# The chunks of an SSD scan in three stages instead of two, with the sample state loaded in mid-group

## The chip, the cores and the metric

The kernel runs on one core of a Trainium2 chip. The metric is the device time of one execution in microseconds (us). The core's engines run side by side and each works through its own instructions in order: PE (TensorE) multiplies matrices and writes to PSUM, DVE (VectorE) and POOL (GpSimd) work elementwise, ACT (ScalarE) computes activations, and SP (SyncE) issues the transfers (DMAs). An instruction that needs what another engine makes waits for a semaphore, and what is queued behind it on its engine waits with it.

## What is computed

One step of a small hybrid encoder: a state-space (SSD) mixer, an MLP, an attention layer and a second MLP, over 1024 prompt tokens and 32 sample tokens of width 1024. The change lies in the SSD mixer, of which the part that matters is the scan over chunks of tokens:

```
def step(h, inp):
    xdt_c, adt_c, b_c, c_c = inp
    a_cs = jnp.cumsum(adt_c, axis=1)
    seg = a_cs[:, :, None] - a_cs[:, None, :]
    decay = jnp.exp(jnp.where(causal[None, :, :, None, None], seg, -jnp.inf))
    cb = jnp.einsum('btgn,bsgn->btsg', c_c, b_c)
    y_diag = jnp.einsum('btsg,btsgr,bsgrp->btgrp', cb, decay, xdt_c)
    y_off = jnp.einsum('btgn,bgrpn,btgr->btgrp', c_c, h, jnp.exp(a_cs))
    decay_end = jnp.exp(a_cs[:, -1:] - a_cs)
    h_new = h * jnp.exp(a_cs[:, -1])[..., None, None] + jnp.einsum(
        'bsgn,bsgr,bsgrp->bgrpn', b_c, decay_end, xdt_c)
    return h_new, y_diag + y_off
```

The state h runs from chunk to chunk of the prompt. The sample tokens start from a state that is an input (h0). There are 8 groups of 4 heads of 64 channels each; a group has its own B and C (128 wide), and its x is two blocks of 128 channels, x0 and x1. B, C, x0 and x1 each come from a projection, a causal convolution of four taps and SiLU. The output y gets D·x added, is multiplied by SiLU(z) (the gate), normalized per group, and projected.

## The kernel before, in words

The scan stage runs from about 83 to 806 us, group by group (g = 0 to 7). A group has nine chunks: eight of 128 prompt tokens, and chunk 8 with the 32 sample tokens. The loop at L601 to L615 makes two lists of small pieces for each g and weaves them (L64 to L76). The main list holds the projections: the two z tiles of group g−1 (`z_tile`), and the four convolution tiles B, C, x0 and x1 of group g+1 (`conv_tile`), with the three pieces of the gate of group g−1 among them. That is 39 pieces in a middle group, and a piece of a projection is 12 matmuls of 128x352. The side list holds the scan of group g (`scan_thunks`), 18 pieces, which are spread evenly, three main pieces behind. Group 0 has the convolutions alone in its main list; group 7 has the z tiles of groups 6 and 7, the gate and the first output projection.

A convolution tile takes three PSUM tiles of 352 columns, which DVE moves out (L400; the last in two parts, L403 and L404). Then `post` runs: the first tap on ACT (L414), two taps on DVE (L416, twice), the last on DVE (L418 and L419), tanh on ACT (L420), and the last product on DVE (L421), whose result, s_4x for block x of group 4, is the operand of group 4's scan. The weights of a projection are split into a high part on ACT (L141) and a low part on POOL (L142). In the gate, PE adds up squares (`ss_g`, L227), DVE takes the inverse root, and L555 scales.

A chunk c of the scan has two stages before. `stage_a(c)` (L453 to L481) loads the cumulated decays (ab), has PE make C·B and three transposes into one PSUM tile (pa, L460 to L463), adds the mask on POOL (L465), takes exp on ACT (L468, four heads), multiplies on DVE (L469, giving L), scales x twice on DVE (L473, giving xd), copies the transposed B on ACT (L476, giving bt), and makes exp(ab)·C on ACT (L478) and POOL (L479). `stage_b(c)` (L483 to L520) makes on PE the state product (L495) into one half of a PSUM bank (tile pb, two buffers), then eight matmuls of outputs into the other half: four with L (L500) and four with the state h of the chunk before (L503). POOL scales the old state (ht, L509), DVE adds the state product (h, L511), and DVE adds D·x to the outputs in place (L514, twice). For chunk 8, the load of h0 is issued in its `stage_b` (L489). The side list runs a(0), a(1), b(0), a(2), b(1) and so on to b(8).

The order in the code is not the order on each engine: a list scheduler of the framework places the instructions of all engines by its own estimate of when they are ready, so a piece that is written at another place can change places with others on its engine. In names, s_3x0 is block x0 of group 3, pb_3_6 is chunk 6 of group 3, and ps_i27 is the projection of column tile 27, which is x1 of group 4 (26 is its x0).

Of the kernel before, what the change touches and what calls it, by code (L numbers as in the profile page):

```python
# [7 lines left out]
F32 = mybir.dt.float32  # L8
# [4 lines left out]
ALU = mybir.AluOpType  # L13
# [28 lines left out]
C_DS = C_AL + 1  # L42
# [50 lines left out]
def hybrid_step(ctx: ExitStack, tc: tile.TileContext, xt, cst, cbf, w_in, w_dt, w_out, w_up0, w_dn0, w_qkv, w_o,  # L93
                w_up1, w_dn1, ssm0, ck, cv, y_o, pssm_o, sssm_o, conv_o, pk_o, v_o):
    nc = tc.nc
    ve, sc, gp, te = nc.vector, nc.scalar, nc.gpsimd, nc.tensor
    dma = nc.sync.dma_start
# [15 lines left out]
    def col(c, n=1):  # L113
        return cs[:, c:c + n]
# [174 lines left out]
    def ssd_layer():  # L289
# [4 lines left out]
        with st:  # L294
            sp = st.enter_context(tc.tile_pool(name="sp", bufs=1))
            qp = st.enter_context(tc.tile_pool(name="qp", bufs=2))
# [89 lines left out]
            slots = {}  # L386
# [60 lines left out]

            def scan_thunks(g):

                out = []  # L450
                box = {}

                def stage_a(c):  # L453
                    w = 128 if c < 8 else 32
                    tk = slice(128 * c, 128 * c + w)
                    B, C, x0, x1 = (slots[g, k] for k in ("B", "C", "x0", "x1"))
                    ab = qp.tile([128, 4, 128], F32, name=f"ab_{g}_{c}", tag="ab", bufs=3)
                    dma(ab[:, :, :w], acs_d[4 * g:4 * g + 4, tk].partition_broadcast(128))
# [3 lines left out]
                    te.transpose(A[0:w, 256:384], x1[:, tk], ident)
                    te.transpose(A[0:w, 384:512], B[:, tk], ident)  # L463
                    L = qp.tile([128, 4, 128], F32, name=f"L_{g}_{c}", tag="L")
                    gp.tensor_tensor(L[0:w, :, :w], ab[0:w, :, :w],  # L465
                                     cs[0:w, None, C_MASK:C_MASK + w].to_broadcast([w, 4, w]), op=ALU.add)
                    for h in range(4):
                        sc.activation(L[0:w, h, :w], L[0:w, h, :w], AF.Exp, bias=naT[0:w, c, 4 * g + h:4 * g + h + 1])  # L468
                    ve.tensor_tensor(L[0:w, :, :w], L[0:w, :, :w], A[0:w, None, 0:w].to_broadcast([w, 4, w]), op=ALU.mult)  # L469
# [6 lines left out]
                    sc.activation(bt[0:w, :], A[0:w, 384:512], AF.Copy)  # L476
                    if c > 0:
                        sc.activation(ab[:, :, :w], ab[:, :, :w], AF.Exp)  # L478
                        gp.tensor_tensor(ab[:, :, :w], ab[:, :, :w],  # L479
                                         C[:, None, tk].to_broadcast([128, 4, w]), op=ALU.mult)  # L480
                    box[c] = (L, xd, bt, ab)  # L481

                def stage_b(c):  # L483
                    w = 128 if c < 8 else 32
                    tk = slice(128 * c, 128 * c + w)
# [9 lines left out]
                    te.matmul(Bp[:, 256:512], bt[0:w, :], xd[0:w, 1, :], start=True, stop=True)  # L495

                    for j in range(2):
                        heads = [(hd, Bp[64 * (hd % 2):64 * (hd % 2) + 64, 128 * j:128 * j + w]) for hd in (2 * j, 2 * j + 1)]
                        for hd, o in heads:
                            te.matmul(o, xd[0:w, 0, 64 * hd:64 * hd + 64], L[0:w, hd, :w], start=True, stop=(h is None))  # L500
                        for hd, o in heads:
                            if h is not None:
                                te.matmul(o, h[:, 64 * hd:64 * hd + 64], ce[:, hd, :w], start=False, stop=True)  # L503
                    hn = qp.tile([128, 256], F32, name=f"h_{g}_{c}", tag="hst", bufs=3)
                    if h is None:
                        ve.tensor_copy(hn, Bp[:, 256:512])
                    else:
                        ht = qp.tile([128, 256], F32, name=f"ht_{g}_{c}", tag="ht", bufs=1)
                        gp.tensor_tensor(ht.rearrange("p (h d) -> p h d", d=64), h.rearrange("p (h d) -> p h d", d=64),  # L509
                                         een[:, 4 * g:4 * g + 4, c, None].to_broadcast([128, 4, 64]), op=ALU.mult)  # L510
                        ve.tensor_tensor(hn, ht, Bp[:, 256:512], op=ALU.add)  # L511
                    for j in range(2):
                        x = slots[g, f"x{j}"]
                        ve.scalar_tensor_tensor(x[:, tk], x[:, tk], col(C_DS + 2 * g + j), Bp[:, 128 * j:128 * j + w],  # L514
                                                op0=ALU.mult, op1=ALU.add)
                    box["h"] = hn
                    if c == 7:
                        dma(pssm_o[g], hn)
                    if c == 8:
                        dma(sssm_o[g], hn)  # L520
# [41 lines left out]
            for d in range(KD):  # L562
                x = hx.tile([128, T], F32, name=f"x0_{d}", tag=f"h{d}")
# [13 lines left out]
            for i, n in enumerate(("ss", "dt", "tails")):  # L577
                ps = p1.tile([128, 512], F32, name=f"p_rstd{i}", tag=n)
                for c in range(2 * i, min(2 * i + 2, 5)):
                    w = 256 if c < 4 else DEC  # L580
# [3 lines left out]
                w = min(512, T - 512 * i)  # L584
# [16 lines left out]
            for g in range(8):  # L601
                main, side = [], scan_thunks(g)
                gt = gate(g - 1) if g > 0 else []
                if g > 0:
                    main += z_tile(g - 1, 0) + z_tile(g - 1, 1)
                if g < 7:
                    for k in ("B", "C", "x0", "x1"):
                        main += gt[0:1] + conv_tile(g + 1, k)
                        gt = gt[1:]
                else:  # L610
                    main += gt[0:1] + z_tile(7, 0) + gt[1:2] + z_tile(7, 1, False) + gt[2:3]
                    out0 = late(lambda: down_block(w_out[0], load_o(yn_d, 0, None, stage(0), 1), X, pg, "o0",
                                                   gmajor=True), 24)
                    main += [lambda: X.extend(load_x(xt, (2, 3, 4, 5, 0, 1, 6, 7), range(2)))] + out0[:6]
                weave(main, side, 2 if g == 7 else 3)  # L615
# [945 lines left out]
    with ExitStack() as st:  # L1561
# [15 lines left out]
        box = {}  # L1577
# [120 lines left out]
```

## Time and profile before

| what | us |
|---|---|
| median of three runs | 3042.72 |
| lowest and highest of them | 3035.66, 3044.68 |
| the profiled execution's own time | 3043.05 |
| its span in the trace | 3041.2 |
| the scan stage (83 to 806): PE busy | 694.54 of 723.00 |
| the same: DVE, ACT, POOL busy | 555.60, 284.32, 445.88 |

The page shows one execution. Busy is the time in which an engine had an instruction under way; matmuls are pipelined, so the time from one's start to the next one's start is shorter than its duration. In a timeline a row gives the start, the duration, the engine, the line, the operation with out<-in, and the count of instructions that it stands for; in brackets is the idle time before it and what ended that.

### The profile page before, as it was taken

The numbers are of one execution on the slowest core, as the hardware profiler recorded it, in microseconds if no ns is written. First come the engines' busy times: TensorE is split into PE (matmuls) and PEld (weight loads), VectorE is DVE, ScalarE is ACT, GpSimd is POOL, SyncE is SP. The second block draws the span as 40 slices with busy tenths as digits, with TensorE's granted clock in tenths as the row PEclk, the third lists the DMA queues.
The fourth block names the chain that finished last, engine by engine and source line by source line (L and its number), as shares of the span: only waits on it lengthen the run. The fifth ranks groups of instructions, "written<-read, shape, count | busy, mean of one in ns | idle before, by whom it ended". The sixth has DMA issues, their size and how long they took to land.

```text
span 3041.2 us, 54987 instructions
## 1 busy us (share of the span) xinstructions
PE 2951.4 (97%) x22206; PEld 2805.2 (92%) x22206; DVE 2272.5 (75%) x3268; ACT 1288.2 (42%) x2207; POOL 768.8 (25%) x591
## 2 busy tenths in 40 slices
PE   9999999999999999999998999999999999999999
PEld 7899888998899999989998988888889999999999
DVE  7877787777847877688777577677777977688776
ACT  4433334333323433344333366666664433344332
POOL 2766666666200211100002023223231211100000
PEclk9999999999999999999999999999999999999999
DMA  4323333233532444375442232222234344375442
GB/s 131 77 68 74 75 84 82 75 73 104 175 117 99 153 152 139 131 252 164 140 128 89 87 81 79 65 76 68 67 117 157 142 156 143 136 254 173 132 139 81
DMA packets 191350, 360.10 MB, mean 118 GB/s; under 512 B 21772, under 2 KB 78968, under 8 KB 191096
## 3 DMA queue, kind: packets, MB, share of 16 engines
q1 hardware_dynamic: 191096, 356.59, 38.2%
q8 instruction: 175, 2.87, 0.4%
q14 instruction: 79, 0.65, 0.1%
HBM read 246.21 MB, written 101.93 MB: 114 GB/s over the span
## 4 chain that ended last, share of the span: by engine, by line
PE 78%; DVE 11%; issue 5%; DMA 3%; ACT 2%; POOL 1%; SPq 0%; DVEq 0%; ACTq 0%; POOLq 0%
PE ps_i L183 13%; PE ps_ua L863 9%; PE ps_ub L863 9%; PE ps_q L183 3%; PE ps_o L183 3%; PE ps_k L183 2%; PE o L1379 2%; PE wt L1363 2%; PE ps_o L164 2%; PE ps_v L183 1%; PE ps_p L183 1%; PE ps_lb L164 1%; PE ps_la L164 1%; DVE p L1326 1%; PE pb L500 1%
## 5 line engine op out<-in xcount | busy, mean ns | idle before, releaser
L183 PE MATMUL ps_i<-xh_n,wh_i 128*128 128x352 f32 x1056 | 360.1, 341 | 0.0
L183 PE MATMUL ps_i<-xh_n,wl_i 128*128 128x352 f32 x1056 | 344.6, 326 | 0.0
L183 PE MATMUL ps_i<-xl_n,wh_i 128*128 128x352 f32 x1056 | 344.5, 326 | 0.0
L1326 DVE TENSOR_TENSOR_SCAN p<-p 128x255 f32<-128x255 f32 (+7 forms) x128 | 193.4, 1512 | 90.7 <-ACT p L1324 89.4
L1328 POOL TENSOR_TENSOR b<-b,p 128x255 f32<-128x255 f32 (+7 forms) x128 | 164.5, 1285 | 379.1 <-DVE p L1326 223.6
L183 PEld LDWEIGHTS ps_i<-xh_n,wh_i 128*128 128x128 f32 x1056 | 202.5, 192 | 13.7 <-issue 11.7
L183 PEld LDWEIGHTS ps_i<-xl_n,wh_i 128*128 128x128 f32 x1056 | 203.7, 193 | 0.0
L183 PEld LDWEIGHTS ps_i<-xh_n,wl_i 128*128 128x128 f32 x1056 | 202.1, 191 | 0.0
L468 ACT ACTIVATE L<-L,naT 128x128 f32<-128x128 f32 (+1 forms) x288 | 89.7, 382 | 164.8 <-POOL L L465 164.8
L1324 ACT ACTIVATE p<-z,qn_q 128x384 f32<-128x384 f32 (+4 forms) x192 | 104.7, 580 | 58.9 <-PE z L1355 29.9
L142 POOL TENSOR_TENSOR wl_i<-ws_i,wh_i 128x1024 fp32r<-128x1024 f32 x44 | 106.5, 2421 | 71.9 <-ACT wh_i L141 71.8
L465 POOL TENSOR_TENSOR L<-ab,cs 128x512 f32<-128x512 f32 (+1 forms) x72 | 103.4, 1437 | 54.9 <-PE pb L500 45.7
L720 ACT ACTIVATE d_b<-y_b 128x528 fp32r<-128x528 f32 x112 | 70.5, 639 | 94.1 <-DMA y_b<-q_db 19.9
L720 ACT ACTIVATE d_a<-y_a 128x528 fp32r<-128x528 f32 x112 | 70.3, 639 | 92.3 <-DMA y_a<-q_da 18.8
L267 POOL TENSOR_TENSOR acc_n<-acc_n,sq_n 128x1056 f32<-128x1056 f32 x6 | 15.8, 2628 | 368.6 <-ACT sq_n L263 368.5
L1363 PE MATMUL wt<-cs,b 128*128 128x128 f32 x576 | 90.3, 280 | 15.4 <-DVE wts L1368 12.8
L1324 ACT ACTIVATE b<-z,qn_q 128x384 f32<-128x384 f32 (+4 forms) x192 | 104.4, 585 | 0.0
L1363 PEld LDWEIGHTS wt<-cs,b 128*128 128x128 f32 x576 | 64.9, 140 | 31.3 <-DVE wts L1368 13.9
L721 DVE TENSOR_TENSOR d_b<-y_b,d_b 128x528 fp32r<-128x528 f32 x112 | 77.7, 704 | 21.3 <-ACT d_b L720 21.3
L721 DVE TENSOR_TENSOR d_a<-y_a,d_a 128x528 fp32r<-128x528 f32 x112 | 77.5, 703 | 21.1 <-ACT d_a L720 21.0
L821 POOL TENSOR_TENSOR wS_a<-ws_a,ws_a 128x512 f32<-128x512 f32 x15 | 33.5, 2236 | 228.7 <-DVE xl_ua L203 145.9
L1366 ACT ACTIVATE wts<-wt 128x512 f32<-128x512 f32 (+3 forms) x128 | 66.6, 520 | 25.2 <-PE wt L1363 23.6
(1650 smaller groups left out, 9568.4 us busy)
## 6 DMA issues: line engine op xcount, KB each, us to landing
y_a<-q_da SPq DMA_DIRECT2D x112, 264.0 KB
y_b<-q_db SPq DMA_DIRECT2D x112, 264.0 KB
ws_i<-in_w_in SPq DMA_DIRECT2D x48, 512.0 KB
ab<-acs_d SPq DMA_DIRECT2D x64, 256.0 KB
q_da<-t_a SPq DMA_DIRECT2D x30, 528.0 KB
q_db<-t_b SPq DMA_DIRECT2D x30, 528.0 KB
ws_a<-in_w_up SPq DMA_DIRECT2D x30, 512.0 KB
ws_b<-in_w_up SPq DMA_DIRECT2D x30, 512.0 KB
```

The lines of the kernel that those rows point to most:

```text
L142: eng[0].tensor_tensor(lo, st, hi.bitcast(F32), op=ALU.subtract)
L164: te.matmul(box["ps"][g][:, :GW], a[:, c:c + 128], b[:, GRP[g]], start=(k == ks[0] and i == 0), stop=(k == ks[-1] and i == 2))
L183: te.matmul(box["ps"][:, :n], a[:, c:c + 128], b[:, grp[g]], start=(k == 0 and i == 0), stop=(k == nk - 1 and i == 2))
L465: gp.tensor_tensor(L[0:w, :, :w], ab[0:w, :, :w], cs[0:w, None, C_MASK:C_MASK + w].to_broadcast([w, 4, w]), op=ALU.add)
L468: sc.activation(L[0:w, h, :w], L[0:w, h, :w], AF.Exp, bias=naT[0:w, c, 4 * g + h:4 * g + h + 1])
L720: sc.activation(hi, x, AF.Copy)
L721: ve.tensor_tensor(lo, x, hi.bitcast(F32), op=ALU.subtract)
L863: te.matmul(ps[:, g, :QW], a[:, c:c + 128], b[:, QW * g:QW * g + QW], start=(first and n == 0 and i == 0), stop=(n == len(ks) - 1 and i == 2),
L1324: sc.activation(t[0:np_, c:c + w], ps[0:np_, :w], AF.Sigmoid, scale=sn[0:np_, f])
L1326: ve.tensor_tensor_scan(p[0:np_, 1:W][:, ::-1], p[0:np_, 1:W][:, ::-1], p[0:np_, 1:W][:, ::-1], 1.0, op0=ALU.mult, op1=ALU.bypass)
L1328: gp.tensor_tensor(b[0:np_, 0:W - 1], b[0:np_, 0:W - 1], p[0:np_, 1:W], op=ALU.mult)
L1363: te.transpose(ps[:, c, :], self.b[:, 128 * (c0 + c):128 * (c0 + c) + 128], ident)
```

## The change

`stage_b` is cut in two. The new `stage_b(c)` has the state product (L497 of the new file), ht (L503) and h (L505); `stage_c(c)` has the outputs (L519 with L, L522 with h) and the two D·x additions (L525). A new piece `bc(c)` runs `stage_c(c-1)` and then `stage_b(c)`. The side list is a(0), a(1), a(2), bc(0), a(3), bc(1) and so on, so the state product is two chunks behind the transposes and the outputs are one more behind; it has 19 pieces. State product and outputs of a chunk stay in one PSUM tile pb, with two buffers. The h0 load has a buffer of its own and is issued in `stage_a(3)`. The buffers: ab 5 instead of 3, L 4 instead of 2, xd 4 instead of 2, bt 3 instead of 2, states 4 instead of 3.

```
@@ stage_a
-                    ab = qp.tile([128, 4, 128], F32, name=f"ab_{g}_{c}", tag="ab", bufs=3)
+                    ab = qp.tile([128, 4, 128], F32, name=f"ab_{g}_{c}", tag="ab", bufs=5)
+                    if c == 0:
+                        box["h0"] = qp.tile([128, 256], F32, name=f"h0_{g}", tag="h0", bufs=1)
                     dma(ab[:, :, :w], acs_d[4 * g:4 * g + 4, tk].partition_broadcast(128))
+                    if c == 3:
+                        dma(box["h0"], ssm0[g])
...
-                    L = qp.tile([128, 4, 128], F32, name=f"L_{g}_{c}", tag="L")
+                    L = qp.tile([128, 4, 128], F32, name=f"L_{g}_{c}", tag="L", bufs=4)
...
-                    xd = qp.tile([128, 2, 256], F32, name=f"xd_{g}_{c}", tag="xd")
+                    xd = qp.tile([128, 2, 256], F32, name=f"xd_{g}_{c}", tag="xd", bufs=4)
...
-                    bt = qp.tile([128, 128], F32, name=f"bt_{g}_{c}", tag="bt")
+                    bt = qp.tile([128, 128], F32, name=f"bt_{g}_{c}", tag="bt", bufs=3)
@@ stage_b
-                    if c == 8:
-                        h = qp.tile([128, 256], F32, name=f"h0_{g}", tag="hst", bufs=3)
-                        dma(h, ssm0[g])
-                    elif c == 0:
-                        h = None
-                    else:
-                        h = box["h"]
+                    h = box["h0"] if c == 8 else box["h"] if c else None
                     Bp = pa.tile([128, 512], F32, name=f"pb_{g}_{c}", tag="pb", bufs=2)
                     te.matmul(Bp[:, 256:512], bt[0:w, :], xd[0:w, 1, :], start=True, stop=True)
-
-                    for j in range(2):
-                        heads = [(hd, Bp[64 * (hd % 2):64 * (hd % 2) + 64, 128 * j:128 * j + w]) for hd in (2 * j, 2 * j + 1)]
-                        for hd, o in heads:
-                            te.matmul(o, xd[0:w, 0, 64 * hd:64 * hd + 64], L[0:w, hd, :w], start=True, stop=(h is None))
-                        for hd, o in heads:
-                            if h is not None:
-                                te.matmul(o, h[:, 64 * hd:64 * hd + 64], ce[:, hd, :w], start=False, stop=True)
-                    hn = qp.tile([128, 256], F32, name=f"h_{g}_{c}", tag="hst", bufs=3)
+                    hn = qp.tile([128, 256], F32, name=f"h_{g}_{c}", tag="hst", bufs=4)
...
+                    box["h"] = hn
+                    box["c", c] = (Bp, h, L, xd, ce)
...
+                def stage_c(c):
+                    w = 128 if c < 8 else 32
+                    tk = slice(128 * c, 128 * c + w)
+                    Bp, h, L, xd, ce = box.pop(("c", c))
+                    for j in range(2):
+                        for hd, o in heads(Bp, j, w):
+                            te.matmul(o, xd[0:w, 0, 64 * hd:64 * hd + 64], L[0:w, hd, :w], start=True, stop=(h is None))
+                        for hd, o in heads(Bp, j, w):
+                            if h is not None:
+                                te.matmul(o, h[:, 64 * hd:64 * hd + 64], ce[:, hd, :w], start=False, stop=True)
                     for j in range(2):
                         x = slots[g, f"x{j}"]
                         ve.scalar_tensor_tensor(x[:, tk], x[:, tk], col(C_DS + 2 * g + j), Bp[:, 128 * j:128 * j + w],
                                                 op0=ALU.mult, op1=ALU.add)
...
+                def bc(c):
+                    if c > 0:
+                        stage_c(c - 1)
+                    if c < 9:
+                        stage_b(c)
 
                 for c in range(9):
                     out.append(lambda c=c: stage_a(c))
-                    if c > 0:
-                        out.append(lambda c=c: stage_b(c - 1))
-                out.append(lambda: stage_b(8))
+                    if c > 1:
+                        out.append(lambda c=c: bc(c - 2))
+                out += [lambda c=c: bc(c) for c in (7, 8, 9)]
                 return out
```

Three places show how the instructions move, all of them at the end of group 3's scan. On PE before, this is the state product of chunk 6 and its outputs, ahead of x1's projection:

```order
L495 MATMUL pb_3_6_4090<-xd_3_6_3949,bt_3_6_3952 128x256 [waits PE_49,Activation_49]
L500 MATMUL pb_3_6_4090<-L_3_6_3942,xd_3_6_3949 64x128 x2
L503 MATMUL pb_3_6_4090<-ab_3_6_3935,h_3_5_3998 64x128 [waits DVE_49]
L503 MATMUL pb_3_6_4090<-ab_3_6_3935,h_3_5_3998 64x128
L500 MATMUL pb_3_6_4090<-L_3_6_3942,xd_3_6_3949 64x128 x2
L503 MATMUL pb_3_6_4090<-ab_3_6_3935,h_3_5_3998 64x128 x2
L183 MATMUL ps_i27_0_4112<-xh_n00_142,wh_i27_4108 128x352 [waits PE_49]
```

and on PE in the new order, from the state product of chunk 7 to the outputs of chunk 6:

```order
L497 MATMUL pb_3_7_4174<-xd_3_7_3981,bt_3_7_3984 128x256 [waits DVE_49,PE_49,Activation_49]
L183 MATMUL ps_i27_1_4151<-xh_n04_262,wh_i27_4105 128x352
L183 MATMUL ps_i27_1_4151<-xl_n04_263,wh_i27_4105 128x352
L519 MATMUL pb_3_6_4132<-L_3_6_3875,xd_3_6_3882 64x128 [waits DVE_49]
L519 MATMUL pb_3_6_4132<-L_3_6_3875,xd_3_6_3882 64x128
L522 MATMUL pb_3_6_4132<-ab_3_6_3868,h_3_5_4026 64x128 [waits Pool_49]
L522 MATMUL pb_3_6_4132<-ab_3_6_3868,h_3_5_4026 64x128
L519 MATMUL pb_3_6_4132<-L_3_6_3875,xd_3_6_3882 64x128 x2
L522 MATMUL pb_3_6_4132<-ab_3_6_3868,h_3_5_4026 64x128 x2
```

The outputs of chunk 6 have moved behind the next chunk's state product and 38 matmuls of x1's projection, and their first matmul has a wait for DVE, for h of chunk 6 (L505), that it had not before.

On DVE before, from the last evictions of x0's projection (tile 26) to the end of its taps:

```order
L403 TENSOR_TENSOR pre0_89<-ps_i26_2_4051,rstd_73 128x320
L404 TENSOR_TENSOR pre0_89<-ps_i26_2_4051,rstd_73 128x32
L511 TENSOR_TENSOR h_3_6_4100<-ht_3_6_4101,pb_3_6_4090 128x256
L514 SCALAR_TENSOR_TENSOR s_3x0_3162<-s_3x0_3162,cs_69,pb_3_6_4090 128x128
L514 SCALAR_TENSOR_TENSOR s_3x1_3313<-s_3x1_3313,cs_69,pb_3_6_4090 128x128
L416 SCALAR_TENSOR_TENSOR cv_4x0_4081<-pre0_89,cwh_138,cv_4x0_4081 128x1059 x2
L418 SCALAR_TENSOR_TENSOR s_4x0_4085<-pre0_89,cwh_138,cv_4x0_4081 128x1024
L419 SCALAR_TENSOR_TENSOR s_4x0_4085<-pre0_89,cwh_138,cv_4x0_4081 128x32
```

and on DVE in the new order, from the same evictions to h of chunk 7:

```order
L403 TENSOR_TENSOR pre0_89<-ps_i26_2_4043,rstd_73 128x320
L404 TENSOR_TENSOR pre0_89<-ps_i26_2_4043,rstd_73 128x32
L416 SCALAR_TENSOR_TENSOR cv_4x0_4094<-pre0_89,cwh_138,cv_4x0_4094 128x1059
L525 SCALAR_TENSOR_TENSOR s_3x0_3175<-s_3x0_3175,cs_69,pb_3_5_4024 128x128
L416 SCALAR_TENSOR_TENSOR cv_4x0_4094<-pre0_89,cwh_138,cv_4x0_4094 128x1059
L525 SCALAR_TENSOR_TENSOR s_3x1_3322<-s_3x1_3322,cs_69,pb_3_5_4024 128x128
L418 SCALAR_TENSOR_TENSOR s_4x0_4098<-pre0_89,cwh_138,cv_4x0_4094 128x1024
L419 SCALAR_TENSOR_TENSOR s_4x0_4098<-pre0_89,cwh_138,cv_4x0_4094 128x32
L505 TENSOR_TENSOR h_3_6_4134<-ht_3_6_4135,pb_3_6_4132 128x256
L400 TENSOR_TENSOR pre1_90<-ps_i27_0_4109,rstd_73 128x352
L505 TENSOR_TENSOR h_3_7_4176<-ht_3_7_4177,pb_3_7_4174 128x256
```

The h of chunk 6 has moved from ahead of x0's taps to behind them, and the outputs of chunk 5 now stand between the taps.

On ACT before, from the tanh of x0 to the first tap of x1 (cv_4x1):

```order
L420 ACTIVATE cv_4x0_4081<-s_4x0_4085 128x1056
L476 ACTIVATE bt_3_8_4155<-pa_3_8_4140 32x128
L468 ACTIVATE L_4_0_4339<-L_4_0_4339,naT_127 128x128 x4
L141 ACTIVATE wh_i30_4532<-ws_i30_4530 128x1024
L414 ACTIVATE cv_4x1_4232<-pre1_90,cwh_138 128x1059
```

and on ACT in the new order, between the same two:

```order
L420 ACTIVATE cv_4x0_4094<-s_4x0_4098 128x1056
L473 ACTIVATE L_4_1_4394<-L_4_1_4394,naT_127 128x128 x4
L483 ACTIVATE ab_4_1_4387<-ab_4_1_4387 128x512
L473 ACTIVATE L_4_2_4442<-L_4_2_4442,naT_127 128x128 x4
L483 ACTIVATE ab_4_2_4435<-ab_4_2_4435 128x512
L141 ACTIVATE wh_i30_4533<-ws_i30_4531 128x1024
L414 ACTIVATE cv_4x1_4241<-pre1_90,cwh_138 128x1059
```

The exponentials of chunks 1 and 2 of group 4 now stand ahead of x1's first tap, where those of chunk 0 stood.

More of the change, by code (lines that the diff above doesn't have):

```diff
@@ L481, in stage_a, with heads @@
                     box[c] = (L, xd, bt, ab)
+                def heads(Bp, j, w):
+                    return [(hd, Bp[64 * (hd % 2):64 * (hd % 2) + 64, 128 * j:128 * j + w]) for hd in (2 * j, 2 * j + 1)]
                 def stage_b(c):
                     w = 128 if c < 8 else 32
-                    tk = slice(128 * c, 128 * c + w)
                     L, xd, bt, ce = box.pop(c)
-                    if c == 8:
-                        h = qp.tile([128, 256], F32, name=f"h0_{g}", tag="hst", bufs=3)
-                        dma(h, ssm0[g])
-                    elif c == 0:
-                        h = None
-                    else:
-                        h = box["h"]
+                    h = box["h0"] if c == 8 else box["h"] if c else None
                     Bp = pa.tile([128, 512], F32, name=f"pb_{g}_{c}", tag="pb", bufs=2)
                     te.matmul(Bp[:, 256:512], bt[0:w, :], xd[0:w, 1, :], start=True, stop=True)
-                    for j in range(2):
-                        heads = [(hd, Bp[64 * (hd % 2):64 * (hd % 2) + 64, 128 * j:128 * j + w]) for hd in (2 * j, 2 * j + 1)]
-                        for hd, o in heads:
-                            te.matmul(o, xd[0:w, 0, 64 * hd:64 * hd + 64], L[0:w, hd, :w], start=True, stop=(h is None))
-                        for hd, o in heads:
-                            if h is not None:
-                                te.matmul(o, h[:, 64 * hd:64 * hd + 64], ce[:, hd, :w], start=False, stop=True)
-                    hn = qp.tile([128, 256], F32, name=f"h_{g}_{c}", tag="hst", bufs=3)
+                    hn = qp.tile([128, 256], F32, name=f"h_{g}_{c}", tag="hst", bufs=4)
                     if h is None:
@@ L511, in stage_b @@
                         ve.tensor_tensor(hn, ht, Bp[:, 256:512], op=ALU.add)
+                    box["h"] = hn
+                    box["c", c] = (Bp, h, L, xd, ce)
+                    if c == 7:
+                        dma(pssm_o[g], hn)
+                    if c == 8:
+                        dma(sssm_o[g], hn)
+                def stage_c(c):
[8 more added lines that the diff above has]
+                                te.matmul(o, h[:, 64 * hd:64 * hd + 64], ce[:, hd, :w], start=False, stop=True)
                     for j in range(2):
@@ L515, in stage_b @@
                                                 op0=ALU.mult, op1=ALU.add)
[L516 to L520, printed above, removed]
+                def bc(c):
[3 more added lines that the diff above has]
+                        stage_b(c)
                 for c in range(9):
                     out.append(lambda c=c: stage_a(c))
-                    if c > 0:
-                        out.append(lambda c=c: stage_b(c - 1))
-                out.append(lambda: stage_b(8))
+                    if c > 1:
+                        out.append(lambda c=c: bc(c - 2))
+                out += [lambda c=c: bc(c) for c in (7, 8, 9)]
                 return out
```

## The prediction

> **What bounds the kernel now.** I read the page first, then PE's waits in the scan stage, then the chain of waits through one group, then the timelines of PE, DVE, ACT and POOL at the end of that group. The page:
>
> ```profile
> span 3041.2 us, 54987 instructions
> PE 2951.4 (97%) x22206; PEld 2805.2 (92%) x22206; DVE 2272.5 (75%) x3268; ACT 1288.2 (42%) x2207; POOL 768.8 (25%) x591
> PE 78%; DVE 11%; issue 5%; DMA 3%; ACT 2%; POOL 1%; SPq 0%; DVEq 0%; ACTq 0%; POOLq 0%
> ```
>
> PE carries most of the chain, so what the change can gain is time in which PE waits or runs at half rate. PE's waits between 110 and 820 us, which is the scan, and the busy time of PE, PEld, DVE, ACT and POOL there, with PE's granted clock:
>
> ```profile
> PE pb L503 <- DMA h<-in_ssm: 10.7, 7, 3.4
> PE pb L503 <- DVE h L511: 9.2, 7, 1.4
> PE pb L495 <- ACT bt L476: 3.2, 7, 1.4
> PE pa L462 <- DVE s_4x L421: 0.5, 1, 0.5
> ...
> 110.00:820.00 710.00, 683.96 (x4765) 633.84 (x4764) 546.21 (x842) 276.23 (x538) 429.90 (x329) 0.98 0.35 87
> ```
>
> The first three are what the change aims at: 10.7 + 9.2 + 3.2 = 23.1 us, three waits in each of seven groups. The fourth is what the next group's first products wait for. Whether the 23.1 us count is read from the chain through group 3's end (start, length, engine, line):
>
> ```profile
> 380.30 0.59 PE ss_g L227 x8
> ...
> 412.80 0.43 DVE pre L400
> ...
> 417.93 1.29 ACT cv_4x L414
> ...
> 429.52 2.26 DMA h<-in_ssm
> 432.81 0.42 DVE h L511
> 433.55 1.48 DVE cv_4x L416
> ...
> 442.10 1.27 DVE s_4x L421
> 443.85 3.84 PE ps_i L183 x24
> ...
> 475.67 0.59 PE ss_g L227 x8
> ```
>
> One group takes 475.67 − 380.30 = 95.37 us. From 412.80 to 443.4 the chain is mainly DVE's: the convolution of head block x0, then the load of the sample state, then the convolution of x1, whose last step L421 releases PE. A wait of PE for h or bt ahead of that does not count if DVE reaches L421 no earlier. So the question is when x1's convolution starts in the new order.
>
> **The change part by part.** DVE before, at that place:
>
> ```profile
> 417.65 0.17 DVE L404 TENSOR_TENSOR pre<-ps_i,rstd 128x32 f32<-128x32 f32 x1
> 417.75 0.41 DVE L511 TENSOR_TENSOR h<-ht,pb 128x256 f32<-128x256 f32 x1
> 418.08 0.59 DVE L514 SCALAR_TENSOR_TENSOR s_3x<-s_3x,cs,pb 128x128 f32<-128x128 f32 x2
> 419.24 4.37 DVE L416 SCALAR_TENSOR_TENSOR cv_4x<-pre,cwh,cv_4x 128x1059 f32<-128x1059 f32 x2 [0.56 <-ACT cv_4x L414]
> 423.64 1.36 DVE L418 SCALAR_TENSOR_TENSOR s_4x<-pre,cwh,cv_4x 128x1024 f32<-128x1024 f32 x1
> ...
> 425.09 0.51 DVE L400 TENSOR_TENSOR pre<-ps_i,rstd 128x352 f32<-128x352 f32 x1
> 425.53 0.26 DVE L469 TENSOR_TENSOR L<-L,pa 32x128 f32<-32x128 f32 x1
> ...
> 426.39 1.94 DVE L421 SCALAR_TENSOR_TENSOR s_4x<-cv_4x,s_4x 128x1056 f32<-128x1056 f32 x1
> ...
> 430.53 0.18 DVE L404 TENSOR_TENSOR pre<-ps_i,rstd 128x32 f32<-128x32 f32 x1
> ```
>
> Before, h of chunk 6 (417.75) stands in the 0.56 us gap that DVE leaves while ACT makes L414. In the new order it stands behind x0's two L416, both outputs of chunk 5, L418 and L419. The outputs of chunk 6 (the first L519) now wait for that h, since the state product and the outputs share one bank and h reads it; before, L500 followed L495 with no wait between them. Queued behind that wait on PE are x1's last matmuls. The prices on PE, before:
>
> ```profile
> 413.62 0.44 PE L503 MATMUL pb<-ab,h 128*64 128x128 f32 x4 [1.43 <-DVE h L511]
> ...
> 415.18 0.49 PE L183 MATMUL ps_i<-xl_n,wh_i 128*128 128x352 f32 x1
> ...
> 417.84 0.32 PE L183 MATMUL ps_i<-xh_n,wl_i 128*128 128x352 f32 x1
> ...
> 424.42 0.59 PE L495 MATMUL pb<-xd,bt 128*128 128x256 f32 x2
> 424.95 0.44 PE L500 MATMUL pb<-L,xd 128*64 128x128 f32 x4
> ...
> 425.97 0.43 PE L183 MATMUL ps_i<-xh_n,wh_i 128*128 128x352 f32 x1
> ```
>
> A state product takes 424.95 − 424.42 = 0.53 us, a chunk's outputs 425.97 − 424.95 = 1.02, and a matmul of the projections 3.84 / 24 = 0.16. Walking group 3's end in before's clock:
>
> 1. The three operations of chunk 8 (425.53 to 426.39, 0.86) now stand ahead of x0's last eviction: 417.75 + 0.86 = 418.6. The outputs of chunk 3 and of chunk 5, each 0.6, enter and leave that stretch of DVE, which comes to nothing.
> 2. L414 on ACT takes until L416 as before, 419.24 − 417.75 = 1.49: 420.1. Then the two L416 4.37, chunk 5's outputs 0.6, L418 and L419 1.45 (423.64 to 425.09), and h 0.33: **426.9**, where it was 418.1.
> 3. PE: outputs of chunk 6 1.02, 22 matmuls 3.5, outputs of chunk 7 1.02, state product of chunk 8 0.53, 12 matmuls 1.9: x1's last matmul ends at about 435.0 and is evicted by 435.6. Before, that was 430.7.
>
> Then ACT sets the start of x1's convolution, since L414 now stands behind two chunks of the next group, not one. ACT before, and the POOL row that feeds it:
>
> ```profile
> 427.25 1.28 ACT L468 ACTIVATE L<-L,naT 128x128 f32<-128x128 f32 x4 [0.41 <-POOL L L465]
> 429.97 1.06 ACT L141 ACTIVATE wh_i<-ws_i 128x1024 fp32r<-128x1024 f32 x1 [1.44 <-PE ps_i L183]
> 430.93 1.25 ACT L414 ACTIVATE cv_4x<-pre,cwh 128x1059 f32<-128x1059 f32 x1
> ...
> 435.12 0.62 ACT L478 ACTIVATE ab<-ab 128x512 f32<-128x512 f32 x1
> ```
>
> ```profile
> 432.62 1.28 POOL L465 TENSOR_TENSOR L<-ab,cs 128x512 f32<-128x512 f32 x1
> ```
>
> The second chunk's mask add takes the L buffer that chunk 7's outputs release (432.5 in step 3): + 1.28 on POOL, exp 1.28, ab 0.62, the weight split 1.06, L414 1.25 = **438.0**, against 433.5 for x1's first L416 before. The row of outputs and L421 behind it is unchanged. So a group's end comes **4.5 us** later, although h0's 2.26 us, bt's and h's waits are gone from it. Its lower bound is DVE's work alone, with PE never late: + 0.86 − 0.6 = +0.3. Its upper one is a stretch of half clock while step 3 runs: the ten matmuls from 415.18 to 417.84 took 2.66 us, not 1.6, so such a stretch costs 1.1 at least, and I take 2, since it began ahead of these rows: 4.5 + 2 = +6.5. I take 4.5, since each step has its own row.
>
> It counts six times (groups 1 to 6): +27. Group 0 has no gate and no z tile beside its scan, so DVE has room; it saves a seventh of the waits, 23.1 / 7 = 3.3, at best, and at worst gets as much in new ones. I take −1. Group 7 has no convolution after it, and its waits are the last of the seven with the longest, 3.4 us: between −4 and +3, I take −1. The new buffers, the h0 load at chunk 3 (one DMA of 2.26 us on SP's queue, moved past the five ab loads behind it, five chunks ahead of its use) and the split of the loop I cost at nothing: nothing on DVE or PE is added by them. Together 27 − 1 − 1 = +25, on the profiled execution's own 3043.05 us (span 3041.2 and 1.85 around it): **3068 us**. That execution is 0.33 above the median of the runs shown, which I leave out. About 0.3%, 9 us, is what a measurement of this kernel can tell from no change; it is also the spread of those runs (3035.66 to 3044.68).
>
> Of that lateness 1.1 us is PE's wait: from x0's last matmul (evicted by 417.65) to L519 it has 38 matmuls, chunk 5's outputs and two state products, 6.1 + 1.0 + 1.1 us, and is there at 425.8, not 426.9.
>
> [...]
>
> [...]
>
> **The rivals.** *Faster.* PE is what bounds, not the DVE chain: the 23.1 us go, and so does the half clock that follows them, at most (1 − 0.98) × 710 = 14 us. For it: PE is 97% busy and every wait named is one that the change gives a chunk of lead. Against: PE's wait for L421 at the group's head stays whatever PE does. It decides if L519 hardly waits. Time: 3043 − 23 − 14 = **3006**. Chance 0.20.
>
> *Same.* The DVE chain itself shrinks. L416 is not always 2.2 us (DVE, then POOL):
>
> ```profile
> 406.96 1.89 DVE L416 SCALAR_TENSOR_TENSOR cv_4C<-pre,cwh,cv_4C 128x1059 f32<-128x1059 f32 x1
> ...
> 409.11 1.30 DVE L416 SCALAR_TENSOR_TENSOR cv_4C<-pre,cwh,cv_4C 128x1059 f32<-128x1059 f32 x1
> ```
>
> ```profile
> 417.94 2.39 POOL L142 TENSOR_TENSOR wl_i<-ws_i,wh_i 128x1024 fp32r<-128x1024 f32 x1
> ```
>
> L416 at 419.24 runs beside POOL's L142 and takes 2.2. If x0's and x1's four L416 fall clear of POOL's work in the new order, each saves up to 0.9, 3.6 in all, and a group end costs 0.9: 6 × 0.9 − 2 = +3, **3046**. [...] Against it: POOL is 430 of 710 us busy, so work shifted by 4 us meets as much of it as before. Chance 0.18.
>
> *Slower*, the forecast, at 0.62: the wait that takes the place of the one removed is PE's for h behind x0's convolution, and the point from which it decides is L416 standing ahead of h on DVE at a group's end.
>
> **How the numbers follow.** Slower by over 0.3%: 0.62, within 0.3%: 0.18, faster: 0.20. The likeliest case's own range goes from six ends midway between 0.3 and 4.5, 3043 + 6 × 2.4 − 2 = 3055, to six at 6.5 with nothing lost elsewhere, 3043 + 39 + 3 = **3085**. Below it the range takes in the same case whole and the upper part of the faster one, in which the waits go and the half clock stays (3043 − 23 = 3020): **3022**. Left out are most of the faster case's 0.20 and a little above 3085.
>
> **What would show it.** Right: PE's waits name L519 or L497 on DVE's h or L525 at the ends of groups 1 to 6; DVE's h of chunk 6 comes right behind L419; L421 of x1 to the group's own ss_g moves by 4 to 5 us, and ss_g to ss_g is about 100 us, not 95.4. The waits for the DMA of in_ssm are gone in either case. Wrong: a period under 95 us, with L519 waiting under 0.3 us, would say that PE bounded after all; a period of 95 to 96 with L416 near 1.4 us would say that POOL's interference carried the price.

## The result and the profile after

Six runs of the changed kernel gave a median of 3059.01 us (3053.54 to 3062.58), six of the kernel before, three of them those shown above, 3039.03: a ratio of 1.0064, 95% interval 1.0049 to 1.0080, or 20 us slower. The forecast was 25 us slower. The profiled execution is the fastest of the six.

The page of the changed kernel:

```profile
span 3051.6 us, 54905 instructions
PE 71%; DVE 13%; issue 6%; ACT 3%; DMA 3%; POOL 2%; SPq 0%; POOLq 0%; DVEq 0%; ACTq 0%
```

PE has lost 7 points of the chain (78% before); DVE, ACT and "issue" have gained them. PE's waits in the scan (us in total, times, the longest), and the busy times there (PE, PEld, DVE, ACT and POOL, then the granted clock, the DMA share and GB/s):

```profile
PE pb L519 <- DVE h L505: 13.0, 14, 1.4
PE pa L467 <- DVE s_1x L421: 3.5, 1, 3.5
...
PE pa L467 <- DVE s_5x L421: 2.7, 1, 2.7
...
PE pb L497 <- DVE s_5x L525: 1.5, 1, 1.5
...
PE pa L467 <- DVE s_4x L421: 1.2, 1, 1.2
...
110.00:820.00 710.00, 669.80 (x4675) 624.51 (x4673) 517.31 (x819) 269.43 (x530) 415.03 (x328) 0.98 0.34 85
```

The three waits that the change aimed at are gone. In their place stand two new ones, for h (L519) and for the D adds that release a tile pb (L497), and the wait for L421 at a group's head has grown from 0.5 to between 1.2 and 3.5 us. The end of group 3, from DVE's timeline:

```profile
425.35 0.17 DVE L404 TENSOR_TENSOR pre<-ps_i,rstd 128x32 f32<-128x32 f32 x1
426.86 1.32 DVE L416 SCALAR_TENSOR_TENSOR cv_4x<-pre,cwh,cv_4x 128x1059 f32<-128x1059 f32 x1 [1.34 <-ACT cv_4x L414]
...
428.36 2.10 DVE L416 SCALAR_TENSOR_TENSOR cv_4x<-pre,cwh,cv_4x 128x1059 f32<-128x1059 f32 x1
...
432.00 0.41 DVE L505 TENSOR_TENSOR h<-ht,pb 128x256 f32<-128x256 f32 x1
...
439.75 0.60 DVE L525 SCALAR_TENSOR_TENSOR s_3x<-s_3x,cs,pb 128x128 f32<-128x128 f32 x2 [2.44 <-PE pb L522]
...
442.90 0.18 DVE L404 TENSOR_TENSOR pre<-ps_i,rstd 128x32 f32<-128x32 f32 x1
...
444.87 2.95 DVE L416 SCALAR_TENSOR_TENSOR cv_4x<-pre,cwh,cv_4x 128x1059 f32<-128x1059 f32 x2 [1.01 <-ACT cv_4x L414]
...
453.50 1.26 DVE L421 SCALAR_TENSOR_TENSOR s_4x<-cv_4x,s_4x 128x1056 f32<-128x1056 f32 x1 [1.15 <-ACT cv_4x L420]
```

and what ACT had ahead of x1's first tap L414, with ss_g of this group and of the next from the chain:

```profile
440.92 1.28 ACT L473 ACTIVATE L<-L,naT 128x128 f32<-128x128 f32 x4 [2.62 <-POOL L L470]
442.11 0.61 ACT L483 ACTIVATE ab<-ab 128x512 f32<-128x512 f32 x1
442.62 1.04 ACT L141 ACTIVATE wh_i<-ws_i 128x1024 fp32r<-128x1024 f32 x1
443.57 1.26 ACT L414 ACTIVATE cv_4x<-pre,cwh 128x1059 f32<-128x1059 f32 x1
```

```profile
389.63 0.58 PE ss_g L227 x8
...
486.33 0.59 PE ss_g L227 x8
```

This stretch starts 389.63 − 380.30 = 9.33 us later than before. Less that shift, the walk of the forecast and what came of it (us in the clock of before):

| step | before | forecast | measured |
|---|---|---|---|
| x0's last eviction done | 417.8 | 418.6 | 416.2 |
| h of chunk 6 done | 418.1 | 426.9 | 423.0 |
| outputs of chunk 7 done | 426.0 | 432.5 | 430.4 |
| x1's last eviction done | 430.7 | 435.6 | 433.8 |
| x1's taps start (L416) | 433.5 | 438.0 | 435.5 |
| x1's L421 done | 443.4 | 447.9 | 445.4 |

The first step moved the other way: x0's last eviction was forecast 0.8 us later and came 1.6 us earlier. The others moved the way that was forecast, each 2 to 4 us less. L421 came 2.1 us later, where 4.5 were forecast, so the 2.4 us missed at the first step are about the whole difference. From ss_g to ss_g a group takes 96.7 us here and 98.3 in groups 2, 4 and 5 (before 95.4), 1.3 to 3.0 more. L421 ends at 65.2 to 65.4 us of the group in all of them; what parts groups 2, 4 and 5 from group 3 is a stretch at half rate right behind L421, at the head of the next group (357.0, 552.3 and 650.7 us, some ten matmuls each); behind the ends of groups 1 and 3 there is none. The end of group 0, forecast at −1, cost 4.9: the first ss_g comes at 194.3, not 189.4. Over the eight groups that is 830.8 − 813.9 = 17 us of the 20.

### The profile page after: what moved, and what is told of

It reads as the page before. It is cut to its first block, busy times and chain, and to the rows that moved or that the text cites. A ratio compares the mean times of both kernels' runs of the same rounds, so it can differ in the third digit from the quotient of the medians.

```text
span 3051.6 us, 54905 instructions
## 1 busy us (share of the span) xinstructions
PE 2950.6 (97%) x22206; PEld 2809.6 (92%) x22206; DVE 2254.7 (74%) x3268; ACT 1287.0 (42%) x2207; POOL 754.9 (25%) x591
## 4 chain that ended last, share of the span: by engine, by line
PE 71%; DVE 13%; issue 6%; ACT 3%; DMA 3%; POOL 2%; SPq 0%; POOLq 0%; DVEq 0%; ACTq 0%
PE ps_ub L875 9%; PE ps_ua L875 9%; PE ps_i L183 8%; PE ps_q L183 3%; PE ps_o L183 3%; PE ps_k L183 2%; PE o L1391 2%; PE wt L1375 2%; PE ps_v L183 2%; PE ps_o L164 2%; PE ps_p L183 1%; PE ps_lb L164 1%; PE ps_la L164 1%; DVE p L1338 1%; DMA ab<-acs_d 1%
## 5 line engine op out<-in xcount | busy, mean ns | idle before, releaser
L473 ACT ACTIVATE L<-L,naT 128x128 f32<-128x128 f32 (+1 forms) x288 | 89.6, 382 | 109.9 <-POOL L L470 109.8
L142 POOL TENSOR_TENSOR wl_i<-ws_i,wh_i 128x1024 fp32r<-128x1024 f32 x44 | 114.4, 2601 | 63.6 <-ACT wh_i L141 63.6
L503 POOL TENSOR_TENSOR ht<-h,een 128x256 f32<-128x256 f32 x64 | 59.5, 929 | 108.0 <-DVE h L505 72.8
```

Of the source, the lines that this page charges most:

```text
L142: eng[0].tensor_tensor(lo, st, hi.bitcast(F32), op=ALU.subtract)
```

## The experiments

Each stands beside runs of the kernel before on the same chip (medians 3040 to 3042). The table measures group 3 in each, from one ss_g to the next: when x1's last eviction ends, its taps start on DVE, L421 ends, and the period, all from the timelines of DVE and PE. Added lines shift the line numbers by a few from kernel to kernel; the names in the rows stay.

| kernel | ratio to before, interval | eviction | taps | L421 | period |
|---|---|---|---|---|---|
| before | 1 | 50.5 | 53.2 | 63.1 | 95.4 |
| changed | 1.0064 (1.0049–1.0080) | 53.5 | 55.3 | 65.2 | 96.7 |
| h0_only | 0.9958 (0.9946–0.9971) | 49.2 | 50.7 | 60.5 | 92.7 |
| h0_bufs | 0.9952 (0.9938–0.9966) | 48.7 | 50.1 | 60.5 | 94.3 |
| lag2 | 0.9987 (0.9978–0.9996) | 49.3 | 52.2 | 62.2 | 94.2 |
| split_lag1 | 1.0030 (1.0019–1.0040) | 52.9 | 54.7 | 64.6 | 95.6 |
| pair | 1.0004 (0.9995–1.0012) | 48.6 | 52.8 | 62.7 | 95.3 |
| lead5 | 1.0077 (1.0064–1.0089) | 59.4 | 61.1 | 71.0 | 99.0 |
| act_late | 1.0017 (1.0007–1.0026) | 52.2 | 53.7 | 64.3 | 95.8 |
| hstt | 1.0099 (1.0082–1.0116) | 51.7 | 57.3 | 65.6 | 98.6 |
| hstt_act_late | 1.0098 (1.0084–1.0111) | 53.3 | 54.7 | 66.1 | 99.0 |
| pair_lead5 | 0.9944 (0.9929–0.9959) | 52.4 | 57.2 | 67.1 | 92.7 |
| pair_lead5_act | 0.9925 (0.9913–0.9937) | 53.1 | 54.5 | 65.3 | 92.7 |
| h0_bufs_act_lead5 | 0.9886 (0.9871–0.9901) | 47.3 | 49.0 | 59.9 | 89.6 |

With three pieces of lead the period is L421's end plus 31 to 34 us in every row: within 3 us, what the group's end loses, the group loses. Where a stretch at half rate follows L421, the period is longer, by 1.6 us in the changed kernel (98.3 and 96.7) and by 2.0 in h0_bufs: there groups 2, 4 and 5 have none and take 92.3 us, group 3 has one at 438.9 and takes the 94.3 of the table.

**h0_only** (the old order, the load early):

```
+                    if c == 3:
+                        dma(box["h0"], ssm0[g])
...
-                        h = qp.tile([128, 256], F32, name=f"h0_{g}", tag="hst", bufs=3)
-                        dma(h, ssm0[g])
+                        h = box["h0"]
```

> The old order with one part of the change: the sample state has its own buffer and is loaded at chunk 3. Theory A (a group's end is set by when x1's convolution starts on DVE): the 2.26 us load goes from the chain; x1's taps start behind its eviction and L414, at about 432.2 instead of 433.47 in group 3, so each of some six group ends comes 1.3 us earlier and group 7 saves its 3.4 us: 9 to 12 us faster than the kernel before, ratio 0.996 to 0.997. Rival B (PE's waits count themselves): the same size, 10.7 us, but PE's wait for L421 at the group's head stays as it is. Rival C (the transfer is hidden anyway): within 3 us of the kernel before.

3027.52 us, 13 faster: theory A's and B's size, and C is out. It does not part A from B, since PE's wait for L421 at the heads of groups 2 to 5 is 0.5 us as it was before. Of the 2.6 us by which taps and L421 came earlier, half is the load and half an earlier eviction. The second half goes with the clock: before, PE ran at half rate ahead of that eviction in groups 1 to 4 (in group 3 from 415.18); in group 5, where the stretch came behind it, the eviction was at 49.2 there too. PE's waits for h are as before:

```profile
PE pb L506 <- DVE h L514: 9.2, 7, 1.4
```

**h0_bufs** (that, with all the new buffers).

> The old order with the early load and all of the new buffers, nothing split. They let ACT and POOL run ahead: the exponentials and ab of chunk 2 of the next group stand ahead of x1's L414 in place of chunk 0's. Theory A with its ACT term as forecast: L414 comes up to 1 us later per group, 0 to 7 us slower than the early load alone (3027.5). Rival I (the buffers carry the 11 us by which the lag of two was slower than the early load alone): 8 to 13 us slower than it.

3026.18 us, as h0_only: the buffers cost nothing, and rival I is out.

**lag2** (the old stage_b, two chunks behind, with the early load and the buffers):

```
-                    if c > 0:
-                        out.append(lambda c=c: stage_b(c - 1))
-                out.append(lambda: stage_b(8))
+                    if c > 1:
+                        out.append(lambda c=c: stage_b(c - 2))
+                out += [lambda c=c: stage_b(c) for c in (7, 8)]
```

> Two chunks of lag without the split: the old stage_b (state product and outputs together, in the old order inside, so that no wait for h lies between them) runs two chunks behind stage_a, with the new buffers and the early load. Theory A: h of chunk 6 stands behind x0's taps here as well and the exponentials of chunks 1 and 2 ahead of L414, so the group's end is late, but PE has one wait less: 5 to 15 us slower than the kernel before. Rival E (the split into two pieces makes the loss): as fast as the kernel before with the early load alone, 9 us faster than before.

3038.58 us, 2 to 4 faster than before and 11 to 12 slower than h0_bufs. Both expectations missed: the lag gives back most of what the early load gained (L421 comes 1.7 us later than in h0_bufs), and from here to the changed kernel, 1.0064, it is the split that costs, with the outputs one more chunk behind.

**split_lag1** (the split, state product one chunk behind).

> The split with a shorter lag: the state product one chunk behind the transposes, as in the old order, the outputs one more. Same tiles, buffers and early load as the changed kernel. Theory A: h of chunk 6 comes ahead of x0's taps again, so the wait of chunk 6's outputs for it goes; the exponentials of chunks 1 and 2 still stand ahead of L414: 3036 to 3046 us, 13 to 23 below the changed kernel. Rival H (it is the later outputs that cost): within 5 us of the changed kernel.

3049.36 us, above A's range and below H's. The wait for h in one bank stays with a shorter lag:

```profile
PE pb L519 <- DVE h L505: 18.6, 9, 2.8
```

**pair** (another pairing in PSUM):

```
                 def bc(c):
+                    Bp = pa.tile([128, 512], F32, name=f"pb_{g}_{c}", tag="pb", bufs=2)
                     if c > 0:
-                        stage_c(c - 1)
+                        stage_c(c - 1, Bp)
                     if c < 9:
-                        stage_b(c)
+                        stage_b(c, Bp)
+                    if c > 0:
+                        add_d(c - 1, Bp)
```

> The changed kernel with another pairing in PSUM: the outputs of chunk c-1 and the state product of chunk c, which PE makes back to back, share a tile pb, in place of state product and outputs of the same chunk. PE then has no wait for h between a state product and its own chunk's outputs, and h of chunk 6 stands between x0's taps instead of behind them. Theory A (PE's wait for h and for L525 at a group's end delays x1's last matmuls): 2 us and more of each group's end go, against the changed kernel 10 to 16 us faster, 3043 to 3049 us. Rival D (the lateness is not PE's wait but the pieces that now stand in x1's stretch and ACT's exponentials ahead of L414): within 4 us of the changed kernel.

3043.16 us, 16 to 18 faster than the changed kernel, as theory A had it. PE's waits now, the whole list but 0.3 us:

```profile
PE pa L467 <- DVE s_7x L421: 5.6, 1, 5.6
PE pa L467 <- DVE s_6x L421: 3.9, 1, 3.9
...
PE pa L467 <- DVE s_1x L421: 3.4, 1, 3.4
```

x1's eviction ends 4.9 us earlier in the group than in the changed kernel, but the taps start only 2.5 earlier, since now ACT is late:

```profile
430.50 0.18 DVE L404 TENSOR_TENSOR pre<-ps_i,rstd 128x32 f32<-128x32 f32 x1
...
434.93 2.96 DVE L416 SCALAR_TENSOR_TENSOR cv_4x<-pre,cwh,cv_4x 128x1059 f32<-128x1059 f32 x2 [3.47 <-ACT cv_4x L414]
```

**act_late** (the changed kernel, ACT's order alone; the exponential of ab is queued in the same way):

```
                     L = qp.tile([128, 4, 128], F32, name=f"L_{g}_{c}", tag="L", bufs=4)
...
+                    with tc.issue_after(slots[g, "x1", "tap0"].ins) if g > 0 and 0 < c < 4 else ExitStack():
+                        for h in range(4):
+                            sc.activation(L[0:w, h, :w], L[0:w, h, :w], AF.Exp, bias=naT[0:w, c, 4 * g + h:4 * g + h + 1])
```

> The changed kernel with one edge on ACT: the exponentials of chunks 1 to 3 of a group are queued behind the first tap L414 of that group's x1 instead of ahead of it. Order on DVE and PE as in the changed kernel. Theory A, as the changed kernel's trace has it: DVE waited at x1 for L414 little longer than L414 itself takes (0.5 us more in group 3, some 2 in group 0), so 3 to 8 us faster than the changed kernel. Rival J (the exponentials are a main part of the lateness, as the forecast's walk had it, 1.1 to 2.4 us per end): 10 to 17 us faster.

3044.19 us, 15 faster: rival J, and theory A's reading of the changed trace was wrong. That reading looked at one group's wait of DVE for L414. The taps started at 55.3 in every middle group, whether x1 was evicted by 53.5 (group 3) or by 52.2 (groups 2, 4 and 5): ACT set them, by little in group 3 and by more than 1 us in the others. With the exponentials behind L414 they start 1.5 us after the eviction:

```profile
434.27 0.18 DVE L404 TENSOR_TENSOR pre<-ps_i,rstd 128x32 f32<-128x32 f32 x1
...
435.96 4.72 DVE L417 SCALAR_TENSOR_TENSOR cv_4x<-pre,cwh,cv_4x 128x1059 f32<-128x1059 f32 x2 [0.74 <-ACT cv_4x L414]
```

The taps come 1.6 us earlier, L421 0.9, since the taps then take 4.72 us and not 2.95. Another part of the gain goes with PE's clock, below.

**hstt** (the changed kernel, DVE's order) wraps h and the D adds in `with tc.high_priority():`.

> The changed kernel with the order on DVE alone changed: h and the D adds are given a high priority, so that at a group's end chunk 5's adds and chunk 6's h stand between x0's two taps instead of behind them. PSUM tiles and the order on PE stay. Theory A (what costs is that DVE comes late to h and to the adds that release pb): half or more of PE's 5 us of waits at a group's end go, 6 to 12 us faster than the changed kernel. Rival G (the shared bank costs by itself, wherever DVE puts h): within 4 us of the changed kernel.

3071.56 us, 11 to 13 slower than the changed kernel: a miss. The eviction came 1.8 us earlier in the group, as A wanted, but the scheduler also put two exponentials of chunk 3 ahead of L414:

```profile
443.38 0.18 DVE L404 TENSOR_TENSOR pre<-ps_i,rstd 128x32 f32<-128x32 f32 x1
449.10 4.09 DVE L416 SCALAR_TENSOR_TENSOR cv_4x<-pre,cwh,cv_4x 128x1059 f32<-128x1059 f32 x2 [5.53 <-ACT cv_4x L414]
```

**hstt_act_late** (both edits).

> The same edge on ACT, on the kernel whose h and D adds stand between x0's taps. That kernel had x1's last matmul 1.8 us earlier in a group than the changed one, but DVE then waited 5.5 us for L414 behind the exponentials of chunk 3 (in the changed kernel 1.3 to 2.4). Theory A with two gates in series (PE's wait for DVE, then ACT's order): with the exponentials out of the way the 4.2 us over L414's own time go at each of seven ends: about 29 us faster than without the edge, 3038 to 3046 us, so the earlier h is worth some 15 us against the changed kernel. Rival G (the shared bank costs by itself): 3055 or more.

3068.43 us: a miss, in rival G's range. DVE's wait fell from 5.53 to 1.40, but the eviction came 1.6 us later in the group than in hstt, and the taps took longer:

```profile
444.21 0.41 DVE L530 SCALAR_TENSOR_TENSOR s_3x<-s_3x,cs,pb 128x32 f32<-128x32 f32 x2 [0.46 <-PE pb L526]
444.53 0.19 DVE L404 TENSOR_TENSOR pre<-ps_i,rstd 128x32 f32<-128x32 f32 x1
446.12 5.21 DVE L417 SCALAR_TENSOR_TENSOR cv_4x<-pre,cwh,cv_4x 128x1059 f32<-128x1059 f32 x2 [1.40 <-ACT cv_4x L414]
```

In both of these kernels L404 ends up behind the D adds of chunk 8, 0.8 us after L403; in the changed kernel it follows L403 at once. So the adds do not part the two. What this kernel has and hstt has not is a stretch at half rate in x1's projection: eight matmuls from 434.5, an estimate of 1 us. So these two runs leave open what an earlier h alone is worth.

**lead5** (`weave(main, side, 2 if g == 7 else 5)` in the changed kernel).

> The changed kernel with the scan's pieces woven five main pieces behind instead of three, so that a group's first products meet x1's L421 two pieces (3.9 us) later. Theory A (the cycle runs through L421 and PE's wait for it at the group's head, 1.2 to 3.5 us in seven groups): these waits go, but the pieces stand closer and come later before x1's end: 10 to 16 us faster than the changed kernel. Rival F (PE is full, the waits at the head only take the place of others): no change within 4 us.

3065.00 us, 4 to 6 more than the changed kernel, which the intervals do not quite part: not A's gain. The waits at the heads of groups 1 to 6 go, but with the pieces closer together the wait for h fills up:

```profile
PE pb L519 <- DVE h L505: 46.0, 19, 4.9
```

**pair_lead5** (the same lead, without that wait).

> The pairing (outputs of chunk c-1 and state product of chunk c in one tile) and the scan's pieces woven five main pieces behind instead of three. With the pairing, PE's only waits in the scan were for x1's L421 at the groups' heads, 3.4 to 5.6 us, 27.8 in all. Theory A: two pieces (3.9 us) more ahead of a group's first products cover them, and no wait for h takes their place: 15 to 25 us faster than the pairing alone, 3018 to 3028 us. Rival F (PE full, or waits reappear at the ends, as with five pieces in the changed kernel): no faster than the pairing, 3043 or more.

3022.05 us, 18 to 21 faster than pair, as A had it. The same edit gains nothing with one pairing and this with the other. The pairing parts them, and with it the wait for h inside the bank, 46.0 us against none.

**pair_lead5_act** (ACT's order as in act_late).

> The pairing with five pieces of lead, and the edge on ACT. DVE waited there 3.2 to 4.6 us for x1's L414, but PE only 0.5 to 1.2 us for L421 at the heads and 4.5 in the last group. Theory A: what PE waited goes, 8 to 10 us: 3012 to 3016. Rival F (PE is nearly full, and the next limit takes its place): within 4 us of 3022.

3017.18 us, a little short of A's range; the intervals of this and pair_lead5 overlap.

**h0_bufs_act_lead5** (no split; early load, buffers, lead, ACT's order).

> The old order of the scan, nothing split, with the early load, the new buffers, five pieces of lead and the edge on ACT. With the load and the buffers alone PE's only waits in the scan were for L421, 1.4 to 3.9 us, 17 in all. Theory A (L421 closes the cycle): two more pieces of lead cover them, 10 to 17 us faster than the load and the buffers alone (3026): 3009 to 3016. Rival K (without the split, waits for bt and h come back at the ends): 3022 or more, and the split pays after all.

3004.78 us, faster than either theory, and the fastest kernel here: 35 us (1.1%) below before. Rival K is out. All of PE's waits in the scan, and its busy times:

```profile
PE pa L467 <- DVE s_7x L422: 2.6, 1, 2.6
PE pb L501 <- ACT bt L482: 0.3, 1, 0.3
...
110.00:820.00 710.00, 707.09 (x5023) 663.67 (x5022) 551.22 (x877) 275.71 (x533) 398.36 (x329) 1.00 0.37 96
```

The waits for h and bt that the split was to remove went without it. Which share lead and ACT's order have in the 21 us over h0_bufs was not measured apart.

## Why the prediction was right, point by point

The direction and the place were right; the size was partly luck. The scan's 17 us are 11.6 at the ends of groups 1 to 6, where 27 were forecast, and 5.3 at groups 0 and 7, where −2 was. Of the signs named, PE's waits carry the names that were forecast, and h of chunk 6 comes right behind L419 (431.84 and 432.00 in the rows above); a period of 100 us did not come. The lower bound of the range, 3022, stops short of the 3020 that it was meant to take in.

*x1's convolution on DVE bounds a group's end, and PE's waits ahead of it are covered.* Shown, to within the 3 us named above: the period follows L421 in every row with three pieces of lead, and pair, whose PE waits nowhere but for L421, is as slow as before.

*h and the D adds stand behind x0's taps, and PE waits for them in the shared bank.* Shown as a wait (L519 13.0 us, and L497), and shown to cost by pair, lead5 and pair_lead5. That the place of h on DVE is the reason is not shown: hstt put h of chunk 6 ahead and gained nothing, though with ACT's order changed too. The runs show what this wait costs, 16 to 18 us together with the changed order on DVE (changed against pair), where the forecast's walk had 1.1 us of it at an end.

*ACT sets the start of x1's taps, through the L buffer that chunk 7's outputs release.* The first half is shown by act_late. The second is not how it went. POOL in group 3 of the changed kernel:

```profile
433.65 1.57 POOL L503 TENSOR_TENSOR ht<-h,een 128x256 f32<-128x256 f32 x1 [0.54 <-DVE h L505]
435.18 1.28 POOL L470 TENSOR_TENSOR L<-ab,cs 128x512 f32<-128x512 f32 x1
438.38 1.28 POOL L484 TENSOR_TENSOR ab<-ab,s_4C 128x512 f32<-128x512 f32 x1 [1.92 <-ACT ab L483]
439.61 1.27 POOL L470 TENSOR_TENSOR L<-ab,cs 128x512 f32<-128x512 f32 x1
```

The second mask add (439.61) follows POOL's own product for chunk 1 without a gap. PE's last read of the buffer had ended at 439.49 here, and in groups 2, 4 and 5 it had ended 1.5 us ahead of the mask add: the buffer was free, POOL was not. From ht of chunk 8 (433.65) to L414 (443.57) POOL and ACT hand the work to and fro, and this takes 9.9 to 10.1 us at the ends of groups 1 to 6; ht starts 44.1 to 44.2 us into each of these groups, whether x1 is evicted by 52.2 or by 53.8. It waits for h of chunk 7 on DVE, behind x0's taps (ht has one buffer, which that h reads). So the late h also reached x1's taps by way of POOL and ACT, which the walk did not have; this is read from the rows, and no run moved it alone. The walk's step took 5.1 us (439.75 to 444.87) for its 5.5 (432.5 to 438.0), but that the outputs were done when POOL came to the mask add is a coincidence of this group.

*4.5 us at six ends.* The term that was mis-sized: 1.3 to 3.0 at five of them, none at the sixth. The walk took DVE's durations of before and let chunk 8's 0.86 us come on top; x0's eviction came 1.6 us earlier instead, since much of DVE's work ahead of it was shorter: from ss_g to this eviction DVE was busy 33.1 us, chunk 8's operations among them, and before 35.9. B's two taps of the same loop, before and after:

```profile
393.56 3.59 DVE L416 SCALAR_TENSOR_TENSOR cv_4B<-pre,cwh,cv_4B 128x1059 f32<-128x1059 f32 x2 [1.31 <-ACT cv_4B L414]
```

```profile
402.40 1.32 DVE L416 SCALAR_TENSOR_TENSOR cv_4B<-pre,cwh,cv_4B 128x1059 f32<-128x1059 f32 x1 [1.97 <-ACT cv_4B L414]
...
404.24 1.32 DVE L416 SCALAR_TENSOR_TENSOR cv_4B<-pre,cwh,cv_4B 128x1059 f32<-128x1059 f32 x1
```

So the rival of no change held a part of the truth: shorter work on DVE gave back about half of the price of an end. That POOL's place is the reason is read from the rows (POOL has a mask add at 394.27 before, and nothing between 401.92 and 405.69 after), and was not tried by itself.

*Group 0 at −1.* Wrong: +4.9. The forecast saw room on DVE, and did not walk ACT there. Before, x1's last eviction began at 142.69 and its taps at 144.75; in the changed kernel:

```profile
147.19 0.18 DVE L404 TENSOR_TENSOR pre<-ps_i,rstd 128x32 f32<-128x32 f32 x1
...
151.38 2.96 DVE L416 SCALAR_TENSOR_TENSOR cv_1x<-pre,cwh,cv_1x 128x1059 f32<-128x1059 f32 x2 [3.25 <-ACT cv_1x L414]
```

In act_late the first ss_g comes at 190.7, so 3.6 of the 4.9 us went with ACT's order, together with the eleven matmuls at half rate (from 162.4 in the changed kernel) that act_late does not have there.

*The early load at nothing on its own.* It was the only part that gained: 13 us alone, which the lag and the split more than gave back.

## What to carry to other kernels

The deeper pipeline did not only remove waits here. It moved work later in the engines' queues (h of chunk 6 on DVE by 4.9 us, 418.1 to 423.0), and what it freed to run early (exponentials with more buffers) got ahead of the step that closes the cycle (act_late took 15 us off): look at each engine's queue at that step. Here it paid (16 to 18 us) that the pieces that share a PSUM bank were those that PE makes back to back, with their readers behind both. Take a change apart before judging it: one small part of this one, the early load, was worth 13 us.

## What the runs showed of the hardware

The half-rate stretches of PE do not follow from the length of one wait. After 2.65 us at the head of group 5 the changed kernel has one:

```profile
551.55 0.48 PE L467 MATMUL pa<-cs,s_5x 128*128 128x128 f32 x1 [2.65 <-DVE s_5x L421]
...
552.33 0.49 PE L183 MATMUL ps_i<-xl_n,wh_i 128*128 128x352 f32 x1
...
554.97 0.32 PE L183 MATMUL ps_i<-xl_n,wh_i 128*128 128x352 f32 x1
```

After 1.2 us in group 4, or 1.7 in act_late, there is none; before had one after 1.43, and h0_only, with the same seven waits for h of up to 1.4, has almost none. In PE's rows between 83 and 830 us, 70 matmuls of 128x352 start at half rate before, 73 in the changed kernel, 20 in act_late and 6 in h0_only; the granted clock over 110 to 820 us is 0.98, 0.98, 1.00 and 1.00. At 0.29 − 0.16 = 0.13 us each, an estimate of 7 us of act_late's 15 and 8 of h0_only's 13 is the clock; the scan's own small matmuls, which fill most of one stretch in group 3 of the changed kernel (432.1 to 435.5), are not in these counts.

The granted clock in the traces of the two kernels shows more. It is 1.00 or 0.50, and each stretch at 0.50 between 85 and 830 us is 3.41 us long or, once in each trace, twice that (in the changed kernel the mean is 0.50 from 551.55 to 554.96). In one trace their starts lie whole multiples of this length apart: before, 61.44 us from 86.38 to 147.82, 18 times 3.413. With the time from 85 to 830 us cut on that grid, 15 pieces at full clock are followed by one at half, and in each of them PE is without a matmul for 1.62 to 2.68 us; in the 400 that are followed by full clock it is for at most 1.56. So in these traces the half clock goes with the idle time summed over such a piece, and not with the length of one wait. Two waits of 1.49 us in the changed kernel show it: the one that ends at 724.18 shares its piece (722.21 to 725.62) with 0.45 us of another, 1.94 in all, and half clock follows; the one that ends at 625.88 is alone in its piece (623.23 to 626.64), and full clock follows. This is read from the traces; no run was made to try it.

The stretches of the profile that the change does not touch, after the last ss_g, took 2221 to 2233 us in the profiled executions of these kernels, so that a span alone can hide more than a third of what the scan lost: the changed kernel's is 10.4 us longer, its scan 17.
